# State-space channels permuted, lag table reversed, convolution adds moved from GpSimd to VectorE, stores moved to ScalarE's queue

## The chip, the cores and the metric

The kernel runs on one core of one Trainium2 chip. The metric is the device time in microseconds (us) of one execution. A core has five engines that run their own instruction queues in order and wait for each other by semaphores: TensorE (PE in the profile), VectorE (DVE), ScalarE (ACT), GpSimd (POOL) and SyncE (SP), which here only issues transfers. A transfer is issued by an instruction in SP's or ScalarE's queue and carried out by the core's 16 DMA engines.

## The reference

One layer of a hybrid trunk on 512 latent tokens of width 1024 with 256 context tokens, all in float32. Cut to its parts:

```python
hx = modulate(rmsnorm(x, g1), shift, scale);  hc = modulate(rmsnorm(ctx, g1), ...)
xa, xb, xcg, ux, qx, kx, vx, gax, gbx, gcx = split_in(hx @ w_in)     # 7 x 512 and 3 x 1024 columns
ya = (xb * depthwise_conv3(xcg * xa, conv_w)) @ conv_out             # A: convolution over tokens
h_f, h_b = complex diagonal scans of B u, both directions, started from the context's states
y = real(C_f h_f + C_b h_b) + d * u                                  # B: 32 groups of 16 channels, 64 states
yb = (gelu(y) @ glu_a) * sigmoid(gelu(y) @ glu_b)
yc = neighbourhood_attention(q, k, v, kc, vc, rpb) @ na_out          # C: 8 heads, window 8 x 16, and the context
x = x + gate * ((sigmoid(ga)*ya + sigmoid(gb)*yb + sigmoid(gc)*yc) @ w_out)
x = x + gate2 * (square(relu(modulate(rmsnorm(x, g2)) @ w1)) @ w2)   # 1024 -> 4096 -> 1024
return rmsnorm(x, gf)
```

## The kernel before

**Weights.** All dense products are done as three products of rounded pieces (lines 99 to 101: high by high, high by low, low by high). A weight block of 128 x 2048 (`raw`, 1 MB) comes by one transfer (line 142) into one of two buffers. Each half of it is a unit's weights: ScalarE rounds it (`wh`, line 171), VectorE takes the rest (`wl`, line 174), and when both halves are used up the block's buffer is free for the next transfer. The units run in the order of `unit_list`: four each of `xa`, `cg`, `xb` and `uc` (the inputs of the convolution and the context's channels of the state space), then the gates `ga` with the products `cv` of the convolution, the gates `gb` and `gc`, then `q`, `k`, `v` with the attention, the products `lb`, `la`, `na`, `wo` and the MLP.

**The convolution.** When a `cg` unit is done, VectorE multiplies it with `xa` (line 941), ScalarE makes three scaled copies (lines 942, 944, 945) and GpSimd adds two of them, moved by a token, to the third: four adds of 504, 7, 7 and 504 columns for each of four units (line 947).

**The state space.** The tokens are cut into 64 chunks of 8. Within a chunk the recurrence is a small dense product, so that the 128 partitions of a tile hold 8 places by 16 channels, and a scan runs over chunks alone. Its tables are made first, in 8 batches of 4 groups: GpSimd makes `e` (lines 455 to 466), TensorE makes the lags `kps` and the turned `etps` from it, which go to DRAM as `KT_d` (15 transfers, lines 483 and 484) and `E_d`; VectorE (batches 0 to 4) and GpSimd (5 to 7) make `c` (lines 495 to 499), which goes to `C_d`. The channels `u` are written to `U_d` (lines 573 and 956). Then class `S5B` goes through 8 batches, and a batch moves between tile and DRAM by 27 transfers: `et`, 8 pieces of `u` (line 629), `ca`, 8 pieces of the lag table `ks` (line 636), 8 pieces of the result `y` (line 710) and its store of `E_d`. A batch's work is a chain over the engines: TensorE `stps` (lines 657, 658), VectorE `A`, `B` (668, 669), GpSimd `v` (674, 675), VectorE 8 scans of `v` (682) and `A2`, `B2` (688, 689), GpSimd `h` (694 to 697), TensorE `yps` (704, 706), ScalarE `y` (708). Beside it GpSimd, VectorE and ScalarE make a table of turns `tb` (643 to 648).

**What sets the order.** The program is written as generators that are advanced between the halves of the units (`slot`, `pump`), and a scheduler of the language then fixes one order of instructions for each engine and queue before the run. In each queue an instruction that waits holds up all behind it. SP's queue holds nearly all transfers: the weight blocks, which wait until their buffer is free, stand in one row with those of the state space.

## Time and profile before

| | |
|---|---|
| time, median of 3 runs | 1063.91 us (1063.01 to 1064.07) |
| the profiled execution | 1062.65 us, of it 1060.9 us from first to last instruction (the span) |
| granted TensorE clock, mean | 0.974 |
| busy share of the span | TensorE 95%, VectorE 52%, ScalarE 35%, GpSimd 21% |
| transfers | 149.41 MB in 70161 packets, 31936 of them under 512 B |

The share of the span in which an engine is busy is a mean over stages. Here the stages differ: in the stretch from 125 to 175 us VectorE and GpSimd are busy nearly without a break, in the second half GpSimd has nothing to do. TensorE's 5% of idle time are few waits, which can be counted one by one. The granted clock is 1.00 or 0.50 of full speed (2.4 or 1.2 GHz) at any moment; a mean of 0.974 is made of some short stretches at 0.50.

### The profile page before, as it was taken

To read this page: it belongs to the slowest core of one execution; us is meant where nothing else is said; L and a number is where in the kernel's file an instruction comes from. 1 tells how busy PE (TensorE), PEld (TensorE's weight loads), DVE (VectorE), ACT (ScalarE), POOL (GpSimd) and SP (SyncE) were. 2 spreads that over 40 slices of the span, in tenths; PEclk is the share of its full clock that TensorE was granted. 3 is DMA by queue.
4 is the path that set the end of the run, shared out by engine and by line. 5 is a ranking of instruction groups with operands and counts; after the bars stand their busy time and mean duration, and the time that the engine had idled before them with its cause. 6 is when DMAs were issued, how large, how long until landed. Compare 5 with 4: busy or idle time off the path is not lost.

```text
span 1060.9 us, 13691 instructions
## 1 busy us (share of the span) xinstructions
PE 1008.4 (95%) x5358; PEld 812.7 (77%) x5358; DVE 553.9 (52%) x911; ACT 371.4 (35%) x594; POOL 225.1 (21%) x175
## 2 busy tenths in 40 slices
PE   5899996999979998999999999999999999999997
PEld 2456885878868886877777778998888888888887
DVE  5734797427945323455467777476443224443322
ACT  4133442423222223354345544246331113343311
POOL 0456298435642222220020200000000000000000
PEclk9999998799969999999999999999999999999999
DMA  7455344856355567442344366223322323223202
GB/s 280 155 190 177 109 170 155 185 181 220 99 158 169 180 224 251 169 160 83 106 153 172 119 227 225 80 80 119 116 83 85 113 80 114 86 90 109 80 1 80
DMA packets 70161, 149.41 MB, mean 141 GB/s; under 512 B 31936, under 2 KB 47296, under 8 KB 57680
## 3 DMA queue, kind: packets, MB, share of 16 engines
q1 hardware_dynamic: 67040, 145.30, 40.7%
q10 hardware_dynamic: 3056, 3.24, 1.0%
q8 instruction: 42, 0.69, 0.3%
q14 instruction: 23, 0.19, 0.1%
HBM read 130.16 MB, written 18.32 MB: 140 GB/s over the span
## 4 chain that ended last, share of the span: by engine, by line
PE 76%; DVE 8%; DMA 6%; SPq 4%; POOL 3%; issue 3%; ACT 1%; DVEq 0%; ACTq 0%; POOLq 0%
PE m L99 10%; PE m L100 10%; PE m L101 10%; PE mod L512 3%; DMA raw<-in_wst_dram 3%; PE ops L831 2%; PE sps L790 2%; SPq L629 2%; PE ptps L816 2%; PE wo L99 1%; PE wo L100 1%; DVE v L682 1%; PE wo L101 1%; DVE wl L174 1%; PE gb L101 1%
## 5 line engine op out<-in xcount | busy, mean ns | idle before, releaser
L174 DVE TENSOR_TENSOR wl<-raw,wh 128x1024 fp32r<-128x1024 f32 x144 | 190.3, 1322 | 226.0 <-ACT wh L171 221.2
L171 ACT CAST wh<-raw 128x1024 fp32r<-128x1024 f32 x144 | 150.8, 1049 | 308.0 <-PE m L100 146.5
L99 PE MATMUL m<-rg,wh 128*128 128x512 f32 (+1 forms) x480 | 184.2, 385 | 0.0
L101 PE MATMUL m<-rg,wl 128*128 128x512 f32 (+1 forms) x480 | 183.9, 384 | 0.0
L101 PEld LDWEIGHTS m<-rg,wl 128*128 128x128 f32 x480 | 90.1, 188 | 19.1
L99 PEld LDWEIGHTS m<-rg,wh 128*128 128x128 f32 x480 | 89.9, 188 | 18.7
L100 PE MATMUL m<-rg,wh 128*128 128x512 f32 (+1 forms) x256 | 96.4, 378 | 0.0
L100 PE MATMUL m<-actl,wh 128*128 128x512 f32 x224 | 87.8, 392 | 0.0
L1070 POOL TENSOR_TENSOR junk<-raw,silx 128x1024 f32<-128x1024 f32 x16 | 46.2, 2886 | 194.8 <-DMA raw<-in_wst_dram 194.8
L100 PEld LDWEIGHTS m<-rg,wh 128*128 128x128 f32 x256 | 48.0, 188 | 8.6
L512 PE MATMUL mod<-raw,cs 128*2 128x256 f32 x128 | 37.1, 452 | 17.0 <-DMA raw<-in_wst_dram 10.0
L100 PEld LDWEIGHTS m<-actl,wh 128*128 128x128 f32 x224 | 42.0, 187 | 9.8
L512 PEld LDWEIGHTS mod<-raw,cs 128*2 128x2 f32 x128 | 11.5, 95 | 37.9 <-issue 17.5
L1025 DVE SCALAR_TENSOR_TENSOR fg<-m,mod,fg 128x512 f32<-128x512 f32 x14 | 10.5, 751 | 52.6 <-PE m L101 52.6
L1074 DVE SCALAR_TENSOR_TENSOR jk<-raw,silx 128x1024 bf16<-128x1024 f32 x16 | 19.6, 1224 | 32.6 <-DMA raw<-in_wst_dram 32.4
L682 DVE TENSOR_TENSOR_SCAN v<-r,v 128x96 f32<-128x96 f32 x64 | 29.3, 522 | 9.4 <-POOL v L674 9.4
L92 ACT CAST rg<-relu 128x512 fp32r<-128x512 f32 (+1 forms) x36 | 20.3, 575 | 38.6 <-DVE relu L1018 38.6
L831 PE MATMUL ops<-pt,v 128*64 128x128 f32 (+1 forms) x256 | 32.5, 288 | 0.0
L93 DVE TENSOR_TENSOR actl<-relu,rg 128x512 fp32r<-128x512 f32 (+1 forms) x36 | 22.3, 632 | 18.6 <-ACT rg L92 18.6
L100 PE MATMUL wo<-rg,wh 128*128 128x256 f32 (+1 forms) x104 | 31.8, 309 | 0.0
L99 PE MATMUL wo<-rg,wh 128*128 128x256 f32 (+1 forms) x104 | 31.8, 307 | 0.0
L1071 ACT ACTIVATE junk<-junk 128x1024 f32<-128x1024 f32 x16 | 17.0, 1063 | 42.1 <-POOL junk L1070 42.1
(428 smaller groups left out, 2351.8 us busy)
## 6 DMA issues: line engine op xcount, KB each, us to landing
raw<-in_wst_dram SPq DMA_DIRECT2D x94, 1024.0 KB, 4.8
E_d<-et SPq DMA_DIRECT2D x8, 512.0 KB, 3.1
C_d<-c SPq DMA_DIRECT2D x8, 512.0 KB, 2.9
et<-E_d SPq DMA_DIRECT2D x8, 512.0 KB, 4.3
ca<-C_d SPq DMA_DIRECT2D x8, 512.0 KB, 3.6
fg<-in_xT_dram SPq DMA_DIRECT2D x4, 512.0 KB, 6.8
raw<-in_wst_dram SPq DMA_DIRECT2D x4, 512.0 KB, 7.7
u<-U_d SPq DMA_DIRECT2D x64, 32.0 KB, 1.8
```

What stands on the lines that cost most here:

```text
L93: (eng or V).tensor_tensor(lo, src, f(hi), op=SUB)
L99: PE.matmul(ps, a[0], b[0], start=start, stop=False)
L100: PE.matmul(ps, a[0], b[1], start=False, stop=False)
L101: PE.matmul(ps, a[1], b[0], start=False, stop=stop)
L171: S.copy(a, src)
L174: V.tensor_tensor(b, src, f(a), op=SUB)
L512: PE.matmul(ps[0:2, 0:256], cs[:, kt], half(h)[:, 256 * (kt % 4):256 * (kt % 4) + 256], start=kt == 0, stop=kt == 7)
L629: nc.sync.dma_start(u[16 * s:16 * s + 16], U_d[s, 64 * q:64 * q + 64].rearrange("(g n) m -> n g m", n=16))
L682: V.tensor_tensor_scan(v[:, g, c], r8, v[:, g, c], 0.0, op0=MUL, op1=ADD)
L790: PE.matmul(ps[:, h, o:o + c1 - c0], q[r, 128 * i:128 * i + 128], k[r, c0:c1], start=True, stop=True)
L831: PE.matmul(ops[r], v[:rows, vt, r], pt[:rows, h, t], start=t == 0, stop=t == 3, skip_group_check=True)
L1070: P.tensor_tensor(junk, half(h), silx, op=MUL)
```

## The change

1. The 512 columns of the projection to `u` (and the rows of the products that take `y`) are permuted on the host, `ug`, so that the partition of a channel in a batch becomes a plain stride in DRAM. `U_d` and `Y_d` get new shapes, and a batch's `u` and `y` become one transfer each instead of 8.
2. The places in a chunk run the other way in the lag table (`c` of the table's loop and the order of the stores), so that `ks` can be read with overlapping rows, by 4 transfers instead of 8. The two halves of the lags `kev` are stored apart; `KT_d` is still written by 15 transfers.
3. The convolution's adds are done by VectorE, in one instruction each that multiplies and adds; the two scaled copies of ScalarE and the adds of GpSimd go.
4. The stores of `E_d` and `U_d` are issued by ScalarE instead of SP.

```diff
@@ table of the state space
-            for lo_, hi_, e, o0, o, c in ((0, 64, slice(6, None, -1), 7, slice(0, 7), slice(0, 8)),
-                                          (64, 128, slice(0, 7), 0, slice(1, 8), slice(7, None, -1))):
+            for lo_, hi_, e, o0, o, c in ((0, 64, slice(6, None, -1), 7, slice(0, 7), slice(7, None, -1)),
+                                          (64, 128, slice(0, 7), 0, slice(1, 8), slice(0, 8))):
...
@@ gen_s5e
-            kev = pool.tile([128, G, 32], F32, name="kev")
+            kev = pool.tile([128, 2, G, 16], F32, name="kev")
...
-                S.copy(kev[:, 4 * b:4 * b + 4], kps)
+                S.copy(kev[:, :, 4 * b:4 * b + 4].rearrange("p e g m -> p g e m"), kps.rearrange("p g (e m) -> p g e m", e=2))
...
-                nc.sync.dma_start(E_d[b], et)
+                nc.scalar.dma_start(E_d[b], et)
...
-            for s in range(8):
-                if s < 7:
-                    nc.sync.dma_start(KT_d[:, :, 16 * (14 - s):16 * (15 - s)].rearrange("g n m -> n g m"), kev[16 * s:16 * s + 16, :, 0:16])
-                nc.sync.dma_start(KT_d[:, :, 16 * (7 - s):16 * (8 - s)].rearrange("g n m -> n g m"), kev[16 * s:16 * s + 16, :, 16:32])
+            for e, s in ((e, s) for s in range(8) for e in range(2) if e or s < 7):
+                i = 16 * (7 * e + s)
+                nc.sync.dma_start(KT_d[:, :, i:i + 16].rearrange("g n m -> n g m"), kev[16 * s:16 * s + 16, e])
...
-        U_d = tc.dram_tile([8, 512, 128], F32, name="U_d")
-        Y_d = tc.dram_tile([512, 8, 64], F32, name="Y_d")
+        U_d = tc.dram_tile([4, 8, 128, 128], F32, name="U_d")
+        Y_d = tc.dram_tile([4, 8, 128, 64], F32, name="Y_d")
...
-            nc.sync.dma_start(U_d[:, 128 * j:128 * j + 128, 32:96].rearrange("a c m -> c a m"), un)
+            nc.scalar.dma_start(U_d[j, :, :, 32:96].rearrange("a c m -> c a m"), un)
@@ S5B
-                for s in range(8):
-                    nc.sync.dma_start(u[16 * s:16 * s + 16], U_d[s, 64 * q:64 * q + 64].rearrange("(g n) m -> n g m", n=16))
+                nc.sync.dma_start(u, U_d[q // 2].rearrange("s (n h g) m -> (s n) h g m", n=16, h=2)[:, q % 2])
...
-                for s in range(8):
-                    nc.sync.dma_start(ks[16 * s:16 * s + 16], KT_d[4 * q:4 * q + 4, :, 16 * (7 - s):16 * (7 - s) + 128].rearrange("g n m -> n g m"))
+                for g in range(4):
+                    a = KT_d[4 * q + g, 0:1, 0:16]
+                    nc.sync.dma_start(ks[:, g], bass.AP(tensor=a.tensor, offset=a.offset, ap=[[16, 8], [240, 16], [1, 128]]))
...
-                for s in range(8):
-                    nc.sync.dma_start(Y_d[64 * q:64 * q + 64, s].rearrange("(g n) m -> n g m", n=16), y[16 * s:16 * s + 16])
+                nc.sync.dma_start(Y_d[q // 2].rearrange("s (n h g) m -> (s n) h g m", n=16, h=2)[:, q % 2], y)
@@ ev_unit, cg and uc
-                t0, t2 = gtile(f"cw0_{j}"), gtile(f"cw2_{j}")
-                S.activation(t0, p, AF.Copy, scale=w0)
-                S.activation(t2, p, AF.Copy, scale=w2)
-                for o, i, n, t in ((8, 0, 504, t0), (1, 504, 7, t0), (0, 8, 504, t2), (504, 1, 7, t2)):
-                    P.tensor_tensor(cv[:, o:o + n], cv[:, o:o + n], t[:, i:i + n], op=ADD)
+                for o, i, n, w in ((8, 0, 504, w0), (1, 504, 7, w0), (0, 8, 504, w2), (504, 1, 7, w2)):
+                    V.scalar_tensor_tensor(cv[:, o:o + n], p[:, i:i + n], w, cv[:, o:o + n], op0=MUL, op1=ADD)
...
-                    nc.sync.dma_start(U_d[:, 128 * j:128 * j + 128, o:o + 32].rearrange("a c m -> c a m"), un)
+                    nc.scalar.dma_start(U_d[j, :, :, o:o + 32].rearrange("a c m -> c a m"), un)
@@ load_g
-                nc.sync.dma_start(yd, Y_d[128 * j:128 * j + 128])
+                nc.sync.dma_start(yd, Y_d[j].rearrange("s c m -> c s m"))
...
-                yv = yd.rearrange("p s (r c) -> p s r c", r=8)
+                yv = yd.rearrange("p s (r c) -> p s r c", r=8)[:, ::-1]
@@ layout, on the host
+    ug = np.arange(512).reshape(4, 8, 16).transpose(0, 2, 1).ravel()
...
```

The scheduler orders the changed program anew, and three places matter. In the rows a number behind a tile's name is the batch (`u0`, `c14` is `c` of batch 4, `e17` is `e` of batch 7) or the running number of a weight block (`raw21`) or weight half (`wl32`).

**SP's queue ahead of the first batch.** Before, from the last store of a context unit's `u` to the first pieces of the lag table:

```order
L956 DMA U_d_619<-uc_sb3_1577 128x8x32 x2
L501 DMA C_d_621<-c16_1535 128x1024
L629 DMA u0_1742<-U_d_619 16x4x128 x8
L629 DMA u1_1786<-U_d_619 16x4x128 x8
L629 DMA u2_1837<-U_d_619 16x4x128 x8
L629 DMA u3_1915<-U_d_619 16x4x128 x8
L142 DMA raw21_1611<-in_wst_dram 128x2048
L501 DMA C_d_621<-c17_1615 128x1024
L142 DMA raw22_1688<-in_wst_dram 128x2048
L626 DMA et0_1740<-E_d_198 128x1024
L626 DMA et1_1784<-E_d_198 128x1024
L633 DMA ca0_1924<-C_d_621 128x1024
```

and in the changed program, at the same place and on to where the pieces of later batches stand behind weight blocks:

```order
L500 DMA C_d_621<-c16_1519 128x1024
L142 DMA raw21_1595<-in_wst_dram 128x2048
L627 DMA u0_1726<-U_d_619 128x512
L627 DMA u1_1763<-U_d_619 128x512
L627 DMA u2_1807<-U_d_619 128x512
L627 DMA u3_1878<-U_d_619 128x512
L142 DMA raw22_1672<-in_wst_dram 128x2048
...
L631 DMA ca1_1989<-C_d_621 128x1024
L708 DMA Y_d_620<-y0_1958 128x256
L635 DMA ks1_1991<-KT_d_199 128x1x128 x4
L142 DMA raw25_2095<-in_wst_dram 128x2048
L627 DMA u5_2099<-U_d_619 128x512
```

The weight block `raw21` now stands ahead of the first four `u`, and these are 4 transfers instead of 32; `u5` stands behind `raw25`.

**VectorE at the end of the `c` tables that it makes.** Before, from the weights of the last `xb` unit to those of the first `uc` unit:

```order
L174 TENSOR_TENSOR wl31_1185<-raw15_938,wh31_1184 128x1024
L421 TENSOR_TENSOR tc40_1335<-cb4_1306,CFai_317 128x512
L93 TENSOR_TENSOR rg7_80<-fg1_82,rg6_79 128x512
L421 TENSOR_TENSOR c14_1308<-cb4_1306,CFar_316 128x512
L421 TENSOR_TENSOR c14_1308<-cb4_1306,CFai_317 128x512
L499 TENSOR_TENSOR c14_1308<-c14_1308,tc40_1335 128x512
L421 TENSOR_TENSOR tc41_1359<-cb4_1306,CFar_316 128x512
L950 TENSOR_TENSOR fg1_82<-xb1_1203,fg0_81 128x512
L499 TENSOR_TENSOR c14_1308<-c14_1308,tc41_1359 128x512
L174 TENSOR_TENSOR wl32_1243<-raw16_1063,wh32_1242 128x1024
```

and in the changed program:

```order
L174 TENSOR_TENSOR wl32_1227<-raw16_1055,wh32_1226 128x1024
L421 TENSOR_TENSOR tc40_1319<-cb4_1290,CFai_317 128x512
L93 TENSOR_TENSOR rg7_80<-fg1_82,rg6_79 128x512
L421 TENSOR_TENSOR c14_1292<-cb4_1290,CFar_316 128x512
L421 TENSOR_TENSOR c14_1292<-cb4_1290,CFai_317 128x512
L498 TENSOR_TENSOR c14_1292<-c14_1292,tc40_1319 128x512
L421 TENSOR_TENSOR tc41_1343<-cb4_1290,CFar_316 128x512
L945 TENSOR_TENSOR fg1_82<-xb2_1241,fg0_81 128x512
L498 TENSOR_TENSOR c14_1292<-c14_1292,tc41_1343 128x512
L174 TENSOR_TENSOR wl33_1280<-raw16_1055,wh33_1279 128x1024
```

The weights of the first `uc` unit (`wl32`) now come ahead of batch 4's table, and those of the second (`wl33`) behind it; the 16 instructions of the convolution (line 942 of the changed program) stand further ahead in this queue.

**GpSimd at the last `e`.** Before, from the last `ta`:

```order
L421 TENSOR_TENSOR ta7_1302<-bc7_1190,CFnci_315 128x512
L421 TENSOR_TENSOR tc50_1452<-cb5_1420,CFai_317 128x512
L421 TENSOR_TENSOR c15_1422<-cb5_1420,CFar_316 128x512
L421 TENSOR_TENSOR c15_1422<-cb5_1420,CFai_317 128x512
L421 TENSOR_TENSOR e17_1301<-bc7_1190,CFcr_314 128x512
L421 TENSOR_TENSOR e17_1301<-bc7_1190,CFnci_315 128x512
L499 TENSOR_TENSOR c15_1422<-c15_1422,tc50_1452 128x512
L457 TENSOR_TENSOR e17_1301<-e17_1301,ta7_1302 128x512
L421 TENSOR_TENSOR tc51_1476<-cb5_1420,CFar_316 128x512
L421 TENSOR_TENSOR tb7_1355<-bc7_1190,CFcr_314 128x512
L499 TENSOR_TENSOR c15_1422<-c15_1422,tc51_1476 128x512
L466 TENSOR_TENSOR e17_1301<-e17_1301,tb7_1355 128x512
```

and in the changed program:

```order
L421 TENSOR_TENSOR ta7_1286<-bc7_1174,CFnci_315 128x512
L421 TENSOR_TENSOR e17_1285<-bc7_1174,CFcr_314 128x512
L421 TENSOR_TENSOR e17_1285<-bc7_1174,CFnci_315 128x512
L457 TENSOR_TENSOR e17_1285<-e17_1285,ta7_1286 128x512
L421 TENSOR_TENSOR tc50_1436<-cb5_1404,CFai_317 128x512
L421 TENSOR_TENSOR tb7_1339<-bc7_1174,CFcr_314 128x512
L466 TENSOR_TENSOR e17_1285<-e17_1285,tb7_1339 128x512
```

The first of GpSimd's own `tc` (`tc50`) still stands ahead of the last step of `e17`, but with one instruction between them instead of nine.

On TensorE the 8 batches move together: from the first `stps` of batch 0 to the first `yps` of batch 7 there stand 440 dense products of lines 99 to 101 before, and 239 in the changed program.

## Rows read from the trace of the kernel before

**Rows 1.** TensorE's waits: for whom, us in total, times, longest us.
```profile
PE kps L435 <- POOL tc L421: 7.5, 1, 7.5
PE k L99 <- ACT tgc L959: 4.2, 1, 4.2
PE stps L657 <- DMA u<-U_d: 4.2, 1, 4.2
PE yps L704 <- DMA ks<-KT_d: 2.9, 2, 2.0
PE ga L99 <- ACT tga L959: 2.3, 1, 2.3
PE kps L435 <- POOL e L466: 1.9, 1, 1.9
```

**Rows 2.** Busy time by stretch: length, PE, PEld, DVE, ACT, POOL, clock, DMA share, GB/s.
```profile
184.40:196.20 11.80, 9.90 (x45) 9.61 (x46) 6.79 (x5) 3.96 (x6) 11.64 (x9) 0.50 0.63 174
237.60:240.60 3.00, 2.99 (x7) 2.42 (x8) 2.47 (x5) 2.39 (x3) 1.98 (x2) 0.50 0.95 307
299.98:315.70 15.72, 13.67 (x69) 11.95 (x70) 5.32 (x10) 2.94 (x6) 7.52 (x8) 0.50 0.59 182
```

**Rows 3.** GpSimd's timeline from 171.9 us: start, us, operation, idle time before.
```profile
172.00 1.98 POOL L421 TENSOR_TENSOR tc<-cb,CFai 128x512 f32<-128x512 f32 x1 [3.76 <-DVE c L499]
...
183.57 1.05 POOL L421 TENSOR_TENSOR tb<-bc,CFcr 128x512 f32<-128x512 f32 x1
...
185.82 2.24 POOL L466 TENSOR_TENSOR e<-e,tb 128x512 f32<-128x512 f32 x1
```

**Rows 4.** GpSimd's groups, 125 to 190 us: count, busy us, mean ns, idle before.
```profile
L947 POOL TENSOR_TENSOR fg<-fg,cw 128x504 f32<-128x504 f32 x8 | 13.7, 1711 | 21.2 <-ACT cw L944 21.2
...
L947 POOL TENSOR_TENSOR fg<-fg,cw 128x7 f32<-128x7 f32 x8 | 4.6, 594 | 0.0
```

**Rows 5.** Busy time while the `c` tables are made, columns as in rows 2.
```profile
125.90:171.90 46.00, 46.00 (x238) 38.10 (x237) 45.39 (x43) 16.24 (x24) 37.19 (x28) 1.00 0.41 152
```

**Rows 6.** VectorE's line 421, 125 to 172 us: shortest, median, longest ns.
```profile
L421 DVE TENSOR_TENSOR tc<-cb,CFai x5: 684/1544/1786, 126.5 to 164.1; 128x512 f32<-128x512 f32 x5
```

**Rows 7.** VectorE's groups over the span, columns as in rows 4.
```profile
L995 DVE SCALAR_TENSOR_TENSOR tlb<-tgb,tlb 128x512 f32<-128x512 f32 x8 | 5.5, 690 | 0.1
...
L258 DVE SCALAR_TENSOR_TENSOR prm<-prm 128x32 f32<-128x32 f32 x12 | 2.3, 190 | 0.2
```

**Rows 8.** The page's costliest group, columns as in rows 4.
```profile
L174 DVE TENSOR_TENSOR wl<-raw,wh 128x1024 fp32r<-128x1024 f32 x144 | 190.3, 1322 | 226.0 <-ACT wh L171 221.2
```

**Rows 9.** SP's queue, 200 to 330 us: start, us, transfers issued.
```profile
213.62 15.79 SPq L629 DMA_DIRECT2D u<-U_d  x32
229.51 0.37 SPq L142 DMA_DIRECT2D raw<-in_wst_dram  x1
...
237.33 7.51 SPq L636 DMA_DIRECT2D ks<-KT_d  x8
```

**Rows 10.** The transfers: count, KB each, median us from issue to landing.
```profile
bt<-in_biasA_dram SPq DMA_DIRECT2D x8, 256.0 KB, 2.8
```

**Rows 11.** VectorE's timeline from 243 us, three of the batches' scans.
```profile
248.25 1.90 DVE L682 TENSOR_TENSOR_SCAN v<-r,v 128x96 f32<-128x96 f32 x4 [0.65 <-POOL v L674]
...
269.84 4.27 DVE L682 TENSOR_TENSOR_SCAN v<-r,v 128x96 f32<-128x96 f32 x8
...
282.00 4.25 DVE L682 TENSOR_TENSOR_SCAN v<-r,v 128x96 f32<-128x96 f32 x8 [0.89 <-POOL v L674]
```

**Rows 12.** Busy time of TensorE's kinds of work, columns as in rows 2.
```profile
243.98:245.52 1.54, 1.54 (x33) 1.35 (x32) 0.00 (x0) 0.78 (x2) 0.73 (x1) 1.00 0.09 20
327.90:330.65 2.75, 2.75 (x26) 2.75 (x25) 2.28 (x4) 1.47 (x2) 2.54 (x2) 1.00 0.49 187
825.00:850.00 25.00, 25.00 (x110) 20.30 (x109) 7.46 (x7) 4.20 (x4) 0.00 (x0) 1.00 0.25 84
```

**Rows 13.** SP's issues of the context units' `u`: shortest, median, longest ns.
```profile
L956 SPq DMA_DIRECT2D U_d<-uc_sb x8: 371/684/2498, 188.3 to 212.0; - x8
```

More of the change, by code (lines that the diff above doesn't have):

```diff
@@ L476, in gen_s5e @@
             nc.scalar.dma_start(dmt, dmat)
-            nc.sync.dma_start(kf0, kev[112:128, :, 0:16])
+            nc.sync.dma_start(kf0, kev[112:128, 0])
             yield
             V.tensor_tensor(kf0, kf0, dmt, op=ADD)
-            V.tensor_tensor(kev[0:16, :, 16:32], kev[0:16, :, 16:32], kf0, op=ADD)
-            for s in range(8):
-                if s < 7:
-                    nc.sync.dma_start(KT_d[:, :, 16 * (14 - s):16 * (15 - s)].rearrange("g n m -> n g m"), kev[16 * s:16 * s + 16, :, 0:16])
-                nc.sync.dma_start(KT_d[:, :, 16 * (7 - s):16 * (8 - s)].rearrange("g n m -> n g m"), kev[16 * s:16 * s + 16, :, 16:32])
+            V.tensor_tensor(kev[0:16, 1], kev[0:16, 1], kf0, op=ADD)
+            for e, s in ((e, s) for s in range(8) for e in range(2) if e or s < 7):
+                i = 16 * (7 * e + s)
+                nc.sync.dma_start(KT_d[:, :, i:i + 16].rearrange("g n m -> n g m"), kev[16 * s:16 * s + 16, e])
             yield
@@ L1362, in half @@
         if kind == "st":
-            r = w_in[256 * j:256 * j + 256, OFF["u"]:OFF["u"] + 512].reshape(2, 128, 512)
+            r = w_in[256 * j:256 * j + 256, OFF["u"]:OFF["u"] + 512][:, ug].reshape(2, 128, 512)
             return r.transpose(1, 0, 2).reshape(128, 1024)
         if kind in ("cv", "lb", "la", "na"):
-            return k4(g[{"cv": "conv_out", "lb": "s5_glu_b", "la": "s5_glu_a", "na": "na_out"}[kind]][0], j)
+            w = g[{"cv": "conv_out", "lb": "s5_glu_b", "la": "s5_glu_a", "na": "na_out"}[kind]][0]
+            return k4(w[ug] if kind in ("lb", "la") else w, j)
+        if kind == "uc":
+            return k8(w_in[:, OFF["u"]:OFF["u"] + 512][:, ug], 128 * j)
         if kind == "wo":
@@ L1374, in half @@
             return k8(g["mlp_w2"][0][r0:r0 + 1024], 128 * m)
-        return k8(w_in, OFF["u" if kind == "uc" else kind] + 128 * j)
+        return k8(w_in, OFF[kind] + 128 * j)
     wst = np.empty((len(STREAM) // 2, 128, 2048), w_in.dtype)
```

## The prediction

> **What bounds the kernel now.** I read the page first (TensorE busy for 95% of the span), then the list of TensorE's waits, then the table of busy time and granted clock by stretch, and only then the timelines of the other engines. With TensorE at 95% the time changes only by what TensorE loses, and it loses in two ways. It waits [rows 1], and behind some waits its clock is granted at 0.50, so that busy time there is worth half [rows 2]. In the list of waits the reader is to see who released TensorE; in the stretches, PE's busy time beside the clock: of b us busy at 0.50, b/2 is lost. The losses that the change can reach lie in three places.
>
> - **Place B, the end of the tables (177 to 196 us).** `kps` waited 7.5 and then 1.9 us for GpSimd [rows 1]; behind it TensorE was busy for 9.90 us at 0.50, which lost 5.0 [rows 2]. Together 14.4 us. GpSimd's timeline tells why: its `tc` waited 3.76 us for VectorE's last `c` and began at 172.00, and the last steps of `e`, which `kps` needs, stood behind it in the queue [rows 3].
> - **Place C, ahead of the first batch (235 to 246 us).** The gate unit `ga` waited 2.3 us for ScalarE's `tga`, which stands behind a weight block's arrival. That block was issued at 229.51, directly behind 32 issues of `u` that held SP for 15.79 us [rows 9]. The first `yps` waited 2.9 − 2.0 = 0.9 us for `ks` [rows 1], whose eight issues took 7.51 us [rows 9], and 2.99 us busy at 0.50 lost 1.5 [rows 2]. Together 4.7 us.
> - **Place D, the batches (296 to 316 us).** `stps` waited 4.2 us for `u`, `yps` 2.0 for `ks` [rows 1], and 13.67 us at 0.50 lost 6.8 [rows 2]. Together 13.0 us.
>
> The wait of `k` for ScalarE's `tgc` (4.2 us) has nothing in the diff that touches it; I leave it as it is.
>
> **The convolution (place B).** Off GpSimd go 13.7 + 4.6 = 18.3 us [rows 4], half of the 37.19 us that it works while the `c` tables are made. In the same 46 us VectorE was busy for 45.39 [rows 5], so here VectorE is the engine that cannot take more, and the change gives it more. No row shows a multiply-and-add of 504 columns there. The nearest are the same operation on 512 columns, 0.69 us, and on 32 columns, 0.19 us [rows 7]: 8 × 0.69 + 8 × 0.19 = 7.0 us. If the new ones are stretched beside GpSimd as `tc` is (below), the 0.69 become 1.54 and the sum 13.8; that is the dear end. The order also shows one `wl` of 1.3 us [rows 8] ahead of batch 4's table that stood behind it. Against this stands what VectorE gets back. Its `tc` took 0.684 us at the shortest and 1.544 in the median [rows 6], while GpSimd worked for four fifths of the time; with half of that gone I give back half of the stretch, 0.43 us each. The ten products of batch 4 and of the end of batch 3, which stand behind the removed work, give 4.3 us; nothing and 8.6 are the ends.
>
> So the last `c` of VectorE, 171.9 before, comes at 171.9 + 7.0 + 1.3 − 4.3 = 175.9 (171.6 to 180.2 as the give-back and the new operations vary, one at its end at a time). Behind it GpSimd still has its `tc`, the `tb` and the last `e` ahead of `kps`: 1.98, 1.05 and 2.24 us [rows 3], together 5.3, or 3.4 if the `tc` and `tb` are done before. `kps` can then start at 179.3 to 181.2, and TensorE is there at 176.9 as before: a wait of 3.4 us (0 to 8.6). A drop of the clock behind it costs 1.5 us as at place C or 5.0 as here, at the most 6.8 as at D [rows 2]; I take 3.5. Place B goes from 14.4 to 6.9: **7.5 us saved**, between 14.4 saved and 1 lost.
>
> Two scaled copies a unit on ScalarE go also; ScalarE is 35% busy and this is worth nothing.
>
> **The transfers ahead of the batches (place C).** The order shows `raw21` ahead of the first four `u`, and these as 4 issues. At 15.79/32 = 0.49 us an issue [rows 9], 28 issues less free SP by 13.8 us, many times the 2.3 that `ga` waited. The four `ks` issues of a batch take half of 7.51, earlier by 3.8 than the 0.9 needed. All of place C goes: **4.7 us saved**. With no wait the drop of the clock has no cause. The other end is that the waits stay and nothing is saved.
>
> Of the Trainium skill one rule speaks against this. "DMA: Bandwidth & Descriptors", section "Issuing engines are not separate DMA queues", says that DMAs initiated elsewhere save only the initiating engine's instruction time, which is usually small beside the DMA itself. By it place C and D would stay as they were; here the issues alone held the queue for 15.79 us, so on this point the trace does not agree. The rival that follows from it is priced below.
>
> **The stores on ScalarE's queue.** ScalarE gets 20 issues (8 of `E_d`, 12 of `U_d`). SP's issues of the context's `u` took 0.37 to 2.50 us, 0.68 in the median [rows 13]; by the median 20 cost 13.7 us, of which few stand ahead of a `wh` that is in haste. I take nothing, hidden by ScalarE's idle 65%. Without that cover, one issue at its longest ahead of one `wh` is 2.5 us on the path; below nothing it cannot come, as ScalarE loses work only in the copies. The load of `yd`, now in shorter rows, and the copy of `kev` in halves stand far from their use and cost nothing; a late `yd` would cost one landing, 2.8 us at the rows' nearest [rows 10].
>
> **The batches (place D).** Here the change does two things. Eight pieces of `u` become one, so SP's queue no longer holds `stps` by its issues. But the scheduler now also puts the eight batches closer together: 239 dense products between the first `stps` and the last `yps` instead of 440. A dense product takes 25.00/110 = 0.227 us, a batch's `stps` 1.54, its `yps` 2.75 [rows 12]. TensorE has 239 × 0.227 + 8 × 4.29 = 88.6 us of work for this stretch. Against it runs the chain of the batches, in which VectorE's scans, its `A2`, `B2`, GpSimd's `h` and the next batch's `v` follow each other, so that a batch costs an interval. From the first scan at 248.25 to the fourth at 282.00 the interval is 11.25 us in the mean, and 12.16 the last [rows 11]. The chain is 4.3 us (243.98, the `stps`, to 248.25, the scan), seven intervals, some 8.5 from the last scan to its `yps` (between the scan alone, 4.25, and an interval), and 2.75: 94.3 to 100.7 us. Where 440 products stood between, this was hidden; now TensorE lacks 5.7 to 12.1 us of work, and I take 8. Where it is lost the order tells: `u5` stands behind the weight block `raw25`, which waits for its buffer, thus for VectorE's `wl`, and that stands behind the scans; then the block's successors do the same. A transfer of 256 KB takes 2.8 us from issue to landing [rows 10], so a late issue is seen by `stps` in full. The ends: 2.5 us (one such landing alone), and 13.
>
> The clock drops behind such waits: 1.5 us behind one of 2.3 (C), 6.8 behind one of 4.2 with one of 2.0 (D) [rows 2]. With two waits I take one of each, 8.3 (1.5 to 13.6). Place D goes from 13.0 to 16.3: **3.3 us lost**, between 9.0 saved and 13.6 lost.
>
> **Sum.** 7.5 + 4.7 − 3.3 = 8.9 us. The profiled execution took 1062.65 us, 1060.9 of it the span, so it becomes 1053.8. The median of the three runs, 1063.91, lies 1.3 above that execution; with the same distance **1055.0 us**.
>
> **The rivals.**
> - *The loop of the batches runs faster and D is free.* Less strain from SP's queue and fewer transfers bring the interval under (88.6 − 15.55)/7 = 10.4 us, and place D loses nothing: 1063.9 − 7.5 − 4.7 − 13.0 = 1038.7. For it: four of an interval's 11.25 us are the scans alone, and the rest has pauses [rows 11]. Against it: `u5` behind `raw25` holds at any interval.
> - *Landing counts and not issue.* The waits at C and D stay as they are and only B gains: 1056.4. For it: a batch's `u` is as many bytes as before, in rows of 128 floats as before. Against it: the 15.79 us of issues [rows 9].
> - *VectorE does not finish earlier at B.* B saves nothing, D loses somewhat: 1063.9 − 4.7 + 3.3 = 1062.5, and up to 1066 with D nearer its end. For it: 45.39 busy of 46.00 us [rows 5]. Against it: GpSimd's waits for ScalarE in the adds (21.2 us) [rows 4] go too.
> - *The loop sets the pace: slower.* With the batches close together each weight half and each piece of the attention's tables that VectorE and GpSimd put between scans and `h` lengthens the interval. At 14 us the chain is 4.3 + 98 + 8.5 + 2.75 = 113.6, 25.0 over TensorE's work, with two long drops of the clock 38.6 in place of 13.0: 1063.9 − 7.5 − 4.7 + 25.6 = 1077.3. It decides from where D takes 25.2 us; with 8.3 of clock that is 16.9 of waiting and an interval of (88.6 + 16.9 − 15.55)/7 = 12.85 us. For it: the last interval read is 12.16 and the intervals grow [rows 11]. Against it: fewer other instructions stand in the same stretch.
>
> **How the numbers follow.** A difference under 0.2% (2.1 us) can't be told from none here. My forecast, with its bounds from 1045 to 1061.8: 0.50; the free loop, 1036 to 1045: 0.17; the landing rule, 1056.4: 0.08; these are faster, 0.75. No gain at B with D somewhat worse, 1061.8 to 1066.0: 0.12. The loop that sets the pace, above 1066.0: 0.13. The range from 1038 to 1066 leaves out some 0.17, most of it above.
>
> **What would show it.** B is right if TensorE's wait ahead of the last `kps`, at about 177 us, is 0 to 8.6 us and GpSimd still releases it; wrong if VectorE's multiply-and-adds are nearer 1.5 than 0.7 us. C is right if no wait for `tga` stands at 235 and the four `u` take SP some 2 us. D is right if TensorE waits for `u` at the sixth or a later batch, with scans 11 to 12.2 us apart and stretches at 0.50 behind it; without such a wait the free loop holds, with intervals above 12.85 the slower one. A new wait on ScalarE's `wh` behind a store would overthrow the zero that I gave its queue.

## The result and the profile after

The changed kernel took 1053.14 us in the median of four runs (1050.4 to 1056.12), the kernel before 1063.99 beside it: a ratio of 0.9896 with a 95% interval of 0.9862 to 0.9929. Six more runs in the study gave 0.9883 [0.9862, 0.9905]. The forecast was 1055.0. The sum was right to 2 us, and most of its terms were not; the section on the prediction goes through them.

TensorE's waits in the changed kernel (line, released by, line: us, times, longest), the answer to [rows 1]:

```profile
PE kps L435 <- POOL e L466: 5.1, 1, 5.1
PE stps L656 <- DMA u<-U_d: 3.5, 1, 3.5
PE yps L703 <- DMA ks<-KT_d: 2.7, 4, 1.8
PE k L99 <- ACT q L964: 2.3, 1, 2.3
PE kps L435 <- issue: 1.9, 1, 1.9
...
PE uc L99 <- DVE fg L945: 1.1, 1, 1.1
PE ga L99 <- ACT tga L954: 0.9, 1, 0.9
```

Its three stretches at a clock of 0.50 between 100 and 400 us, columns as in [rows 2]:

```profile
184.70:192.00 7.30, 7.30 (x34) 7.30 (x35) 1.52 (x2) 1.32 (x2) 6.96 (x6) 0.50 0.20 76
236.40:239.80 3.40, 3.40 (x26) 2.88 (x23) 2.33 (x5) 0.00 (x0) 1.96 (x3) 0.50 0.90 345
278.40:291.00 12.60, 12.31 (x65) 10.96 (x66) 10.40 (x20) 2.96 (x7) 8.19 (x10) 0.50 0.59 169
```

No place is free of waits. The wait for `kps` is 1.9 + 5.1 us where it was 7.5 + 1.9, and the wait for `u` 3.5 where it was 4.2. The `ga` that waits is an earlier gate unit than before, at 216.6 us and not at 237.6. What is new in the list is the kind of `k`'s wait: ScalarE's `q` and no more its `tgc`, 2.3 us and not 4.2.

To compare kernels I added up, for each place, all of TensorE's idle time and half of its busy time at a clock of 0.50. The places reach from 100 us to 12 us behind the last `kps` (tables), from there to 1 us before the first `stps` (ahead), on to the last `yps` (batches), and on to 430 us (gates and `k`). In us, from one profiled execution each:

| | span | tables | ahead | batches | gates, `k` |
|---|---|---|---|---|---|
| before | 1060.9 | 15.6 | 3.8 | 15.3 | 6.1 |
| changed | 1052.7 | 13.5 | 0.9 | 14.2 | 5.4 |
| changed, second profile | 1050.7 | 10.5 | 4.1 | 12.4 | 4.0 |
| changed, convolution on GpSimd | 1045.0 | 14.6 | 0.0 | 10.1 | 3.0 |
| the same, second profile | 1048.7 | 15.8 | 0.0 | 10.9 | 3.1 |

The four places explain 6.8 of the changed kernel's 8.2 us and 9.8 of 10.2 in its second profile. The tables gave 2.1 and 5.1 us, the place ahead 2.9 and −0.3, the batches 1.1 and 2.9, the last place 0.7 and 2.1; no place gave the bulk in both. Two profiles of one kernel differ by up to 3.2 us at a place, and there is one profile of before, so a gain of a microsecond or two at one place is not shown by itself.

### The profile page after: what moved, and what is told of

It is laid out like the page before. It is cut to its first block, busy times and chain, and to the rows that moved or that the text cites. A ratio compares the mean times of both kernels' runs of the same rounds, so it can differ in the third digit from the quotient of the medians.

```text
span 1052.7 us, 13485 instructions
## 1 busy us (share of the span) xinstructions
PE 1004.4 (95%) x5358; PEld 810.2 (77%) x5358; DVE 558.9 (53%) x927; ACT 366.7 (35%) x586; POOL 200.7 (19%) x159
## 4 chain that ended last, share of the span: by engine, by line
PE 74%; DMA 8%; DVE 8%; POOL 5%; issue 3%; ACT 2%; SPq 1%; ACTq 0%; DVEq 0%; POOLq 0%
PE m L99 10%; PE m L100 10%; PE m L101 10%; PE mod L511 3%; PE ops L829 2%; DMA raw<-in_wst_dram 2%; DMA C_d<-c 2%; PE sps L788 2%; PE ptps L814 2%; PE wo L100 1%; PE wo L99 1%; PE wo L101 1%; DVE v L681 1%; DVE wl L174 1%; DMA ks<-KT_d 1%
## 5 line engine op out<-in xcount | busy, mean ns | idle before, releaser
L174 DVE TENSOR_TENSOR wl<-raw,wh 128x1024 fp32r<-128x1024 f32 x144 | 187.6, 1303 | 226.1 <-ACT wh L171 224.4
L511 PE MATMUL mod<-raw,cs 128*2 128x256 f32 x128 | 35.0, 432 | 17.9 <-DMA raw<-in_wst_dram 10.9
L511 PEld LDWEIGHTS mod<-raw,cs 128*2 128x2 f32 x128 | 11.2, 92 | 38.1 <-issue 15.9
L1069 DVE SCALAR_TENSOR_TENSOR jk<-raw,silx 128x1024 bf16<-128x1024 f32 x16 | 21.8, 1362 | 32.5 <-DMA raw<-in_wst_dram 32.5
L1020 DVE SCALAR_TENSOR_TENSOR fg<-m,mod,fg 128x512 f32<-128x512 f32 x14 | 10.5, 751 | 52.8 <-PE m L101 52.8
L101 PE MATMUL wo<-rg,wl 128*128 128x256 f32 (+1 forms) x104 | 31.5, 306 | 0.0
```

The source lines that it names most:

```text
L101: PE.matmul(ps, a[1], b[0], start=False, stop=stop)
L174: V.tensor_tensor(b, src, f(a), op=SUB)
L511: PE.matmul(ps[0:2, 0:256], cs[:, kt], half(h)[:, 256 * (kt % 4):256 * (kt % 4) + 256], start=kt == 0, stop=kt == 7)
L1069: V.scalar_tensor_tensor(jk, half(h), 1.0, silx, op0=MUL, op1=MUL, accum_out=modx[:, i:i + 1])
```

## The experiments

All ratios are against the kernel before, run on the same chip in turn; 0.2% is what they can tell at best, and mostly it is 0.25% to each side.

| | median us | ratio, 95% |
|---|---|---|
| convolution on VectorE alone | 1064.01 | 0.9990 [0.9973, 1.0007] |
| stores on ScalarE alone | 1057.52 | 0.9928 [0.9903, 0.9952] |
| changed | 1052.57 | 0.9883 [0.9862, 0.9905] |
| changed, stores on SP | 1053.81 | 0.9887 [0.9865, 0.9909] |
| changed, all in 8 pieces | 1063.35 | 0.9980 [0.9961, 1.0000] |
| changed, `u` alone in 8 pieces | 1050.15 | 0.9860 [0.9838, 0.9883] |
| changed, convolution on GpSimd | 1048.91, 1050.27 | 0.9858 [0.9831, 0.9886], 0.9849 [0.9828, 0.9870] |
| changed, buffer of its own for `tc` | 1054.30 | 0.9908 [0.9878, 0.9937] |
| the same with four `cb` | 1050.96 | 0.9860 [0.9839, 0.9880] |
| the same, convolution on GpSimd | 1052.32 | 0.9875 [0.9852, 0.9898] |
| changed, five `u` | 1054.62 | 0.9886 [0.9848, 0.9923] |

**The changed kernel again.** No edit.

> The changed kernel once more, for a second profile and a narrower interval. By the places (theory 1: the time is what TensorE loses at the tables, ahead of the batches and in the batches) the gain is about 10 us (1050 to 1056) and the second profile again shows a wait of 3 to 7 us ahead of the last kps with a stretch at 0.50 behind it, and one wait of stps for u5 of some 3.5 us with a stretch at 0.50 behind it. By the rival (theory 2: these waits differ from run to run, and the gain with them) the second profile lacks one of the two waits, or the gain is under 5 us.

Measured 1052.57 us. The second profile has both waits: 1.9 + 5.1 us for `kps`, 2.4 for `u`. Theory 1 stands, as far as it says where TensorE waits.

**The convolution alone.** In the kernel before:

```diff
-                t0, t2 = gtile(f"cw0_{j}"), gtile(f"cw2_{j}")
-                S.activation(t0, p, AF.Copy, scale=w0)
-                S.activation(t2, p, AF.Copy, scale=w2)
-                for o, i, n, t in ((8, 0, 504, t0), (1, 504, 7, t0), (0, 8, 504, t2), (504, 1, 7, t2)):
-                    P.tensor_tensor(cv[:, o:o + n], cv[:, o:o + n], t[:, i:i + n], op=ADD)
+                for o, i, n, w in ((8, 0, 504, w0), (1, 504, 7, w0), (0, 8, 504, w2), (504, 1, 7, w2)):
+                    V.scalar_tensor_tensor(cv[:, o:o + n], p[:, i:i + n], w, cv[:, o:o + n], op0=MUL, op1=ADD)
```

> The kernel before with part 3 alone: the convolution's adds on VectorE, all transfers as before. Theory 1: the place of the tables goes from 14.4 us lost to about 11.8, as in the changed kernel (waits of 1.1 + 1.9 + 5.1 and 3.7 by the clock), and the other places stay: 2 to 3 us faster than before, about 1061.4. Theory 2, that VectorE has no room: the 11.2 us that the convolution takes there push the last c back by as much, and it is slower than before by up to 5 us. Theory 3, that this part makes the whole gain: about 1053.

Measured 0.9990: no difference that can be told. The tables lost 10.6 us instead of 15.6, more gain than expected; the place ahead of the batches lost 6.9 instead of 3.8, the batches 17.4 instead of 15.3 and the last place 7.4 instead of 6.1, which takes it back. Its list of waits (columns as above) and SP's queue (start, us, transfers issued):

```profile
PE stps L657 <- DMA et<-E_d: 7.9, 1, 7.9
...
PE kps L435 <- POOL e L466: 5.1, 1, 5.1
PE k L99 <- ACT tgc L956: 4.6, 1, 4.6
```

```profile
211.98 19.64 SPq L629 DMA_DIRECT2D u<-U_d  x32
...
234.75 0.80 SPq L626 DMA_DIRECT2D et<-E_d  x2
```

TensorE came to the first `stps` earlier, and `et0` stood behind the 32 issues of `u` and a store of `c`. Before, TensorE came there later, after its longer wait at the tables, and `et0` was no wait.

**The convolution back on GpSimd.** The changed kernel with the diff above reversed, measured twice.

> The changed kernel without part 3: the convolution's adds on GpSimd again, transfers, permutation and stores as changed. Theory 1: the tables lose 14.4 us as before, the batches gain what they did (3 to 4 us) and more if u5 is in time, since here the order puts u5 ahead of raw25: 4 to 10 us faster than before, 1054 to 1060. Theory 2, that the convolution alone matters: 1064, as before. Theory 3, that the transfers alone matter: 1050 to 1053.

> The changed kernel with the convolution on GpSimd once more, to narrow its interval and to see a second profile. If the convolution on VectorE costs the changed kernel something by the order that comes with it: again 3 to 5 us faster than the changed kernel, 1047 to 1050. If it is neutral: 1051 to 1055. If it saves the 7.5 us of the prediction: 1058 to 1061.

Measured 0.9858 and 0.9849. Without the convolution's move the change gains more, about 15.5 us instead of 12; but the interval of the changed kernel begins at 0.9862 and those of this version end at 0.9886 and 0.9870. That the move costs the changed kernel something is likely and not shown. Its waits, in the first of the two profiles:

```profile
PE kps L435 <- POOL tc L421: 7.5, 1, 7.5
...
PE yps L703 <- ACT tb L645: 3.7, 1, 3.7
PE kps L435 <- POOL e L466: 1.9, 1, 1.9
PE yps L703 <- DMA ks<-KT_d: 1.6, 2, 1.3
```

The tables lose what they lost before, the `ga` and `u` waits are gone, and the table above shows where the changed kernel is worse: ahead, in the batches and at `k`, together some 7 us by the means, against some 3.2 better at the tables.

**A buffer of its own for GpSimd's `tc`.**

```diff
-                    ta = pool.tile([128, 512], F32, tag="tc", name=f"tc{b}{c}")
+                    ta = pool.tile([128, 512], F32, tag="tc" if b < 5 else "tcp", name=f"tc{b}{c}")
```

> The changed kernel with a buffer of its own for GpSimd's tc, so that tc of batch 5 need not wait for VectorE's last c. Theory 1: GpSimd ends the last e some 7 us earlier, the wait of TensorE ahead of the last kps (1.9 + 5.1) and the clock behind it (3.7) go, and, as the order now also puts u5 ahead of raw25, the wait of 3.5 for u5 and its clock (6.4) may go too: 8 to 20 us faster than the changed kernel, 1034 to 1045. Rival: the last e is late because of its own load from DRAM and the weights; the wait for kps stays over 4 us and the time within 3 us of the changed kernel's.

Measured 0.9908, no gain. GpSimd's timeline (start, us, idle time before and who ended it) shows a new wait in place of the old one:

```profile
172.00 1.29 POOL L421 TENSOR_TENSOR tc<-cb,CFai 128x512 f32<-128x512 f32 x1 [4.64 <-DMA cb<-in_s5bc_dram]
173.26 1.50 POOL L421 TENSOR_TENSOR e<-bc,CFcr 128x512 f32<-128x512 f32 x1
```

The `tc`, which no more waited for VectorE, was put ahead of all of the last `e`, and there it waited for its input from DRAM. The rival named the load of `e`; it was that of `cb`.

**The same with four buffers for `cb`**, so that this load is early, and then **with the convolution on GpSimd**, where the order in the batches is the same:

```diff
-                t = pool.tile([128, 128], F32, tag="cb", bufs=2, name=f"cb{b}")
+                t = pool.tile([128, 128], F32, tag="cb", bufs=4, name=f"cb{b}")
```

> The changed kernel with a buffer of its own for GpSimd's tc and four buffers instead of two for cb, so that tc of batch 5 waits neither for VectorE's last c nor for the load of cb; u5 stands ahead of raw25 here too. Theory 1: the last e is done when TensorE comes to the last kps, the waits of 1.9 + 5.1 us and the clock behind them (3.5 to 3.7) go, so 7 to 11 us less than the changed kernel at the tables: 1040 to 1047. Rival: GpSimd's chain of c (one buffer, a store between) ends no earlier, and what is won at the tables is given back at the first batches: 1050 to 1054.

> The same two buffers' changes with the convolution back on GpSimd: on SP and in the batches on TensorE the order is the same as in the version with the convolution on VectorE (tc_cb), so the two differ by the convolution alone. Theory 1 (the convolution moves only the end of the tables): its 18 us on GpSimd make the last e late by some us, and it is 2 to 6 us slower than tc_cb. Rival 1 (the convolution's 11 us on VectorE cost of themselves): 3 to 5 us faster than tc_cb. Rival 2 (once nothing waits for VectorE's last c it doesn't matter where it is): within 2 us of it.

Measured 0.9860 and 0.9875. The wait for `kps` is 1.9 us in the first and 1.8 in the second, and the tables lose 7.0 and 5.3 us instead of 10 to 16. Little of it reaches the end, since the first batches now wait for GpSimd. TensorE's waits with the convolution on VectorE:

```profile
PE yps L705 <- POOL h L695: 3.7, 1, 3.7
PE stps L656 <- POOL rr L644: 3.0, 1, 3.0
PE yps L703 <- DMA ks<-KT_d: 3.0, 3, 1.4
PE kps L435 <- issue: 1.9, 1, 1.9
```

Neither version is told from the other, as the second rival said: as far as these runs can tell, it doesn't matter which engine adds where nothing waits for VectorE's last `c`.

**Five buffers for `u`.**

```diff
-                u = self.tl("u", q, [128, 4, 128], bufs=4)
+                u = self.tl("u", q, [128, 4, 128], bufs=5)
```

> The changed kernel with five buffers for u instead of four: the order then has u4 ahead of the first batches and u5 ahead of the weight block raw25, and all else as it was. Theory 1 (the order costs, not VectorE): the wait of stps for u5 (2.4 to 3.5 us) and the stretch at 0.50 behind it (5 to 6.4 us lost) go, 5 to 9 us faster than the changed kernel, 1044 to 1048, level with the version that has the convolution on GpSimd (1048.9). Rival (the chain of the batches is the limit whoever holds u): the wait turns up at yps, for h or ks, and the time stays within 3 us of the changed kernel's 1052.6.

Measured 0.9886, with single runs from 1046.8 to 1062.3 us. No `stps` waits for `u` any more; `yps` waits for `ks` instead:

```profile
PE yps L703 <- DMA ks<-KT_d: 8.5, 4, 4.2
```

This is what the rival named, in the place of the wait and in the median. Why `ks` was late the longest time (4.2 us, until 287.28) can be read from SP's and ScalarE's queues:

```profile
286.12 0.32 SPq L708 DMA_DIRECT2D Y_d<-y  x1
286.49 1.84 SPq L635 DMA_DIRECT2D ks<-KT_d  x3
```

```profile
284.40 0.52 ACT L645 ACTIVATE tb<-rr 128x384 f32<-128x384 f32 x1 [8.36 <-POOL rr L644]
```

Three of the four pieces of `ks` stand behind the store of the last batch's `y`; ScalarE copied that `y` at 285.74, though TensorE had made it by 278.9, since the copy stood behind a `tb` for which ScalarE sat idle for 8.36 us until GpSimd's `rr`. So at this wait it is again the order of a queue, and not the chain as the prediction counted it.

**`u` in 8 pieces of the same layout.**

```diff
-                nc.sync.dma_start(u, U_d[q // 2].rearrange("s (n h g) m -> (s n) h g m", n=16, h=2)[:, q % 2])
+                for s in range(8):
+                    nc.sync.dma_start(u[16 * s:16 * s + 16], U_d[q // 2, s].rearrange("(n h g) m -> n h g m", n=16, h=2)[:, q % 2])
```

> The changed kernel with each batch's u loaded in 8 pieces of 16 partitions, from the same permuted layout, so the bytes and rows are the same and only the issues are eight times as many. Theory 1 (issues hold SP's queue): 32 issues take some 13 to 16 us ahead of the first batch, the waits for the blocks behind them and for u and ks come back, 4 to 10 us slower than the changed kernel, 1056 to 1063. Rival (landing counts, not issue): within 2 us of the changed kernel, 1051 to 1055.

Measured 0.9860: no slower than the changed kernel, and 6 to 13 us under what theory 1 had. SP's queue (columns as above) shows that the issues did hold it:

```profile
216.54 16.70 SPq L628 DMA_DIRECT2D u<-U_d  x32
...
233.80 1.22 SPq L142 DMA_DIRECT2D raw<-in_wst_dram  x2
236.44 1.11 SPq L625 DMA_DIRECT2D et<-E_d  x2
```

The four issues of the changed kernel took 1.75 us, the block behind them followed at 219.84 and the first `et` at 227.83. Both came later here, and the first `stps` began at 244.3 us instead of 232.0. The time did not suffer, because this is not a change of the issues alone: the new order also puts the batches later among the dense products on TensorE (252 instead of 206 between the last `kps` and the first `stps`). What 32 issues cost in the changed kernel's own order is not shown.

**All in 8 pieces, the stores alone, and the stores back on SP.** The first has `u` as above, and `ks` and `y` alike; the other two swap `nc.sync` and `nc.scalar` in the stores of `E_d` and `U_d`:

```diff
-                for g in range(4):
-                    a = KT_d[4 * q + g, 0:1, 0:16]
-                    nc.sync.dma_start(ks[:, g], bass.AP(tensor=a.tensor, offset=a.offset, ap=[[16, 8], [240, 16], [1, 128]]))
+                for g, h in ((g, h) for g in range(4) for h in range(2)):
+                    a = KT_d[4 * q + g, 0:1, 64 * h:64 * h + 16]
+                    nc.sync.dma_start(ks[64 * h:64 * h + 64, g], bass.AP(tensor=a.tensor, offset=a.offset, ap=[[16, 4], [240, 16], [1, 128]]))
...
-                nc.sync.dma_start(Y_d[q // 2].rearrange("s (n h g) m -> (s n) h g m", n=16, h=2)[:, q % 2], y)
+                for s in range(8):
+                    nc.sync.dma_start(Y_d[q // 2, s].rearrange("(n h g) m -> n h g m", n=16, h=2)[:, q % 2], y[16 * s:16 * s + 16])
```

> The changed kernel with the permuted layouts but all of a batch's u, ks and y in 8 pieces each, 27 transfers as before; the stores are on ScalarE and the convolution on VectorE. The order puts the batches as far apart on TensorE as before (607 instructions from the first stps to the last yps, 634 before). Theory 2 (the number of transfers): about the time of before, 1060 to 1065, and k waits 4 us again. Theory 1 (stores, or the layout itself): within 3 us of the changed kernel, 1050 to 1056.

> The kernel before with part 4 alone: the stores of E_d and U_d issued by ScalarE, all 27 transfers a batch as they were, the convolution on GpSimd. Theory 1 (the stores in SP's queue held up what stood behind them, above all the loads ahead of the first batches): the wait of ga for tga and the clock behind it go, 3 to 8 us faster than before. Theory 2 (the number of a batch's transfers makes the gain, for it lets the batches end 50 us earlier and leaves the stage of k alone): within 2 us of before, with the wait of k for tgc of some 4 us still there.

> The changed kernel without part 4: the stores stay on SP, everything else as changed. Theory 1 (stores): loses what the stores gave, 3 to 8 us slower than the changed kernel, 1056 to 1061. Theory 2 (the number of transfers): within 2 us of the changed kernel, 1051 to 1055, with a wait of k under 2.7 us.

Measured 0.9980, 0.9928 and 0.9887. With 8 pieces for all three most or all of the gain is gone, as theory 2 said, though stores and layout are the changed ones (it is `gc` and not `k` that waits, 5.4 us). The stores alone gain 0.7%, as theory 1 said, though they too leave 27 transfers a batch; so the 27 pieces by themselves do not undo the gain. These two versions also differ by the convolution, the layout and the order. Taking the stores' move away from the changed kernel loses nothing, as theory 2 said: either the stores or the other parts are enough ahead of the batches, where 0.0 us are lost with the stores alone and 0.1 with the stores back on SP. The queue of SP with the stores alone shows it (columns as above):

```profile
207.71 0.35 SPq L142 DMA_DIRECT2D raw<-in_wst_dram  x1
210.49 18.09 SPq L629 DMA_DIRECT2D u<-U_d  x32
228.68 0.37 SPq L501 DMA_DIRECT2D C_d<-c  x1
```

There are 32 issues of `u` still, and they take 18.09 us; but the block that `tga` needs is issued at 207.71, ahead of them, and no `ga` waits. Before it was issued at 229.51 [rows 9].

Why 8 pieces of all three cost and 8 of `u` alone do not is not shown; SP's queue in the batches suggests one reason. In the version with all in 8 pieces (columns as above):

```profile
276.02 0.42 SPq L710 DMA_DIRECT2D Y_d<-y  x1
276.49 0.42 SPq L628 DMA_DIRECT2D u<-U_d  x1
276.95 0.42 SPq L710 DMA_DIRECT2D Y_d<-y  x1
...
280.19 4.39 SPq L636 DMA_DIRECT2D ks<-KT_d  x8
```

The issues follow each other every 0.46 us, `y` and `u` in turn. A batch's 26 on SP fill 26 × 0.46 = 12.0 us, which is longer than the changed kernel's interval of 11.1 us between the scans of two batches; with `u` alone in pieces they are 15, or 6.9 us, and the queue has room. That is an estimate from these rows, and it cannot be the whole reason, since in this version the scans come 14.9 us apart in the mean. What is shown is only that the version with `ks` and `y` in pieces too takes 10 to 13 us more; which of the two, and how much of it is the order that the scheduler makes of it (the batches end at 395.5 us in this version and at 338.5 in the changed one), is open.

## Why the prediction came out, step by step

- **The convolution (7.5 us saved at the tables): about twice too large there, and for the kernel nothing that can be told, perhaps a loss.** The tables lost 2.1 and 5.1 us less in the two profiles. In the prediction's own terms, `kps` waited 1.9 + 5.1 = 7.0 us in both and not 3.4, and the clock behind it cost 3.7 and 3.5, as priced: 3.8 and 4.0 us saved. Two things were mis-sized. VectorE's new operations took 7.9 + 3.3 = 11.2 us, not 7.0 (groups of line, count, busy, mean ns; 125 to 200 us):

```profile
L942 DVE SCALAR_TENSOR_TENSOR fg<-fg,vec,fg 128x504 f32<-128x504 f32 x8 | 7.9, 981 | 0.0
...
L942 DVE SCALAR_TENSOR_TENSOR fg<-fg,vec,fg 128x7 f32<-128x7 f32 x8 | 3.3, 422 | 0.0
```

  And the give-back came but was spent on waiting. `tc` took 0.78 us in the mean and not 1.40, but as `c` has one buffer, VectorE then waited for its store, 5.1 us in three waits where it had been 0.4. GpSimd waited 9.17 us for the last `c` (the two timelines: start, us, idle time before):

```profile
152.75 1.11 DVE L421 TENSOR_TENSOR c<-cb,CFar 128x512 f32<-128x512 f32 x1 [3.57 <-DMA C_d<-c]
...
165.85 1.37 DVE L421 TENSOR_TENSOR c<-cb,CFar 128x512 f32<-128x512 f32 x1 [1.11 <-DMA C_d<-c]
...
178.18 0.68 DVE L498 TENSOR_TENSOR c<-c,tc 128x512 f32<-128x512 f32 x1
```

```profile
168.10 1.73 POOL L457 TENSOR_TENSOR e<-e,ta 128x512 f32<-128x512 f32 x1
179.00 1.91 POOL L421 TENSOR_TENSOR tc<-cb,CFai 128x512 f32<-128x512 f32 x1 [9.17 <-ACT rg L92]
...
182.45 2.13 POOL L466 TENSOR_TENSOR e<-e,tb 128x512 f32<-128x512 f32 x1
```

  The last `c` ended at 178.9, not at 175.9, within the stated bounds. (The upper one, 180.2, was itself too low: the dear end of the new operations, 13.8 us, makes 182.7.) The releaser that the profile names at 179.00, ScalarE's `rg`, had been done; that the wait was for VectorE's `c`, whose `tc` buffer this one takes, the version with a buffer of its own shows, in which another wait ended it. The larger error is that a gain at the tables was counted as a gain of the kernel. With the convolution alone it was handed back at the next places but for a microsecond that can't be told from nothing, and in the changed kernel a part is handed back at `ga`, as the next point shows.
- **The transfers ahead of the batches (4.7 saved): almost nothing was saved, and the cause was half right.** What was predicted of the queue came: `raw21` was issued at 210.97 instead of 229.51, the four `u` took 1.75 us, and no `ga` waits at 237. But `ga` now waits one weight block earlier, 0.9 us and 2.2 in the second profile. ScalarE's `wh`, behind which `tga` stands, waited until 214.99 for the block issued at 206.50, which comes no earlier than before (205.89), while TensorE came to this `ga` at 215.7 and 213.5 us instead of 218.8. That is time won at the tables and handed back (SP's and ScalarE's queues, columns as above):

```profile
206.50 1.13 SPq L142 DMA_DIRECT2D raw<-in_wst_dram  x1
...
210.97 0.53 SPq L142 DMA_DIRECT2D raw<-in_wst_dram  x1
216.69 1.75 SPq L627 DMA_DIRECT2D u<-U_d  x4
```

```profile
214.99 1.05 ACT L171 CAST wh<-raw 128x1024 fp32r<-128x1024 f32 x1 [3.80 <-DMA raw<-in_wst_dram]
```

  In the first profile the first `yps` also waited 1.8 us for `ks`, with 1.7 of clock behind it (the table above counts both to the batches); in the second the clock behind `ga` cost 1.7. So of the 4.7 us that the prediction wanted to save, 4.4 and 3.9 were still lost. Nor is the number of issues shown to be the cause: with the stores alone the place loses nothing with 32 issues in it, as `raw21` stands ahead of them. With the convolution alone `raw21` stands ahead of them too (211.27), and there `et0`, behind the 32 issues, came too late. In the prediction I held the row of 15.79 us [rows 9] against the Trainium skill's rule ("DMA: Bandwidth & Descriptors", section "Issuing engines are not separate DMA queues") that issue time is usually small beside the DMA itself. The wait of 7.9 us for `et0` behind 19.64 us of issues does not agree with it here; the time of the version with `u` in 8 pieces does, though in another order.
- **The batches (3.3 lost): the direction was wrong, the mechanism partly there.** The place lost 14.2 and 12.4 us where it had lost 15.3. The wait for `u5` behind `raw25` came, 3.5 and 2.4 us, with 12.31/2 = 6.2 and 4.6 us of clock behind it. SP's queue in the first profile:

```profile
272.15 0.33 SPq L142 DMA_DIRECT2D raw<-in_wst_dram  x1
272.59 0.38 SPq L627 DMA_DIRECT2D u<-U_d  x1
```

  The `stps` that waited began at 278.32, 5.7 us after the issue of its `u5` and not the 2.8 that I took for a landing: directly behind a 1 MB block the transfer itself took longer, and the wait is not only a late issue. The second wait that I had priced did not come: `raw26` was issued at 297.65 and `u7` at 298.08, in time. All waits in the batches came to 4.3 and 5.6 us, where I had taken 8. The intervals between batches, from the first scan to the last (VectorE's timeline), are (314.95 − 237.45)/7 = 11.1 us, just under the 11.25 that I had as the lower end:

```profile
237.45 1.88 DVE L681 TENSOR_TENSOR_SCAN v<-r,v 128x96 f32<-128x96 f32 x4 [1.85 <-POOL v L673]
...
314.95 2.89 DVE L681 TENSOR_TENSOR_SCAN v<-r,v 128x96 f32<-128x96 f32 x8 [2.07 <-POOL v L673]
```

- **`k` (nothing): missed.** It gave 0.7 and 2.1 us, and 3.0 without the convolution's move. The batches end at 338.5 us instead of 395.2, and ScalarE has another order in the stage of `gc` and `k`. In both kernels the wait goes back to a weight block. Before, `tgc` stood on ScalarE behind `junk` (a product with the block that the modulation needs), which waited for GpSimd's `junk` on that block; in the changed kernel ScalarE waits for a block itself, for `wh`, and `q` comes ahead of `tgc` (before, then changed):

```profile
417.90 1.06 ACT L1071 ACTIVATE junk<-junk 128x1024 f32<-128x1024 f32 x1 [8.89 <-POOL junk L1070]
...
410.73 1.99 ACT L171 CAST wh<-raw 128x1024 fp32r<-128x1024 f32 x2 [4.15 <-DMA raw<-in_wst_dram]
```

  That the new order comes from the earlier end of the batches is my reading, and not shown. With all in 8 pieces the batches end at 395.5 and this place loses 7.6 us.
- **The stores (nothing): right beside the other parts (0.9887 without them, 0.9883 with them), wrong for the stores alone** (0.9928). ScalarE's `wh` did stand once behind two stores (208.22 us, idle 1.73 ahead of it), the sign that was to overthrow the zero, but no wait of TensorE followed from it.
- **The rivals.** The loop that sets the pace did not come. That the loop be free did not either: it held to its 11 us and TensorE waited in the batches, for `u` or, with five buffers, for `ks`. The landing rule had C and D as they were; C was, nearly, and B gained about half of what that rival left it.

So the total came out by luck. In the prediction's own terms the tables and the place ahead of the batches were taken some 8 us too high; against that stood the batches, where 3.3 us were to be lost and 1 to 3 were gained, and `k`, whose wait was to stay and fell by 1.6 to 1.9.

The version with the lowest ratios leaves the convolution on GpSimd and keeps the other parts: 1048.91 and 1050.27 us. Its intervals overlap those of several others.

## What to carry to other kernels

A wait that is taken away pays only as far as the next engine in line is ready: before a stage's gain is added to the sum, read when the next stage's inputs come, and what hides behind the old wait. When transfers are cut up or merged, count the issues of a queue per round of the loop and set them beside the round's time, and read what stands behind them: here 32 issues stood ahead of a wait of 7.9 us in one version and of none in two others, by what came next in the queue and when it was needed. Look also at the order of the other engines, which an edit of the transfers can change as well. And when several edits relieve one queue, their gains need not add.

## What was not expected of the hardware

The mean of 422 ns for a multiply-and-add of 7 columns hides two kinds: six took 0.21 to 0.22 us and two 1.02 and 1.07. Of 504 columns six took 0.73 to 0.74 us and two 1.61 and 1.84. The four long ones began while a GpSimd instruction ran, the other twelve did not. With 7 columns, all six long ones of the two profiles of the changed kernel ended 0.02 to 0.03 us after the end of a GpSimd instruction, as here at 156.27 and 156.24:

```profile
154.74 1.50 POOL L421 TENSOR_TENSOR e<-bc,CFnci 128x512 f32<-128x512 f32 x1
155.25 1.02 DVE L942 SCALAR_TENSOR_TENSOR fg<-fg,vec,fg 128x7 f32<-128x7 f32 x1
```

So the stretch was 0.8 to 1.1 us an operation at both sizes. The prediction's dear end stretched all of the 504 columns and none of the 7; in the run a quarter of each was stretched.

Executions of one kernel spread more than the three runs of before had shown: 1046.8 to 1062.3 us with five buffers for `u`, 1060.9 to 1069.4 for the kernel before over the study. A part arises at the very start, where the kernels do the same: TensorE's wait for `sq` began between 16.7 and 19.9 us.
